# A hybrid encoder layer on one core: the second part of each weight block is made by GpSimd where the lanes run

## The chip, the core and the metric

The kernel runs on one core of a Trainium2 chip. The core has a matrix engine (TensorE, in the profile PE, with its weight loads as PEld), a vector engine (VectorE, DVE), a scalar engine (ScalarE, ACT), a general engine of parallel processors (GpSimd, POOL) and an engine that only issues transfers (SyncE, SP). The metric is the device time of one execution in microseconds, as the median of several.

## What is computed

One layer of a bidirectional encoder with three parallel groups of heads, on two requests (1024 and 256 tokens of width 2048) that share the weights:

```
def layer(x, mem, ...):
    proj = rms_norm(x, norm_g) @ w_in
    xbc, z_ssd, dt_raw, q, k, v, z_att, mq, z_mem = split_cols(proj, IN_SIZES)
    xs, Bm, Cm = split(silu(centred_dwconv(xbc)))
    y = ssd_scan(xs, forward) + ssd_scan(xs, backward) + d_skip * xs
    o_ssd = rms_norm(y * silu(z_ssd))
    o_att = window_attention(rms_norm(q), rms_norm(k), v, sink) * silu(z_att)
    mk, mv = split(rms_norm(mem) @ w_mem_kv)
    o_mem = softmax(rms_norm(mq) @ rms_norm(mk).T) @ mv * silu(z_mem)
    return x + concat[o_ssd, o_att, o_mem] @ w_out
```

Everything is in 32-bit floats.

## The kernel before

**Split products.** TensorE multiplies in a rounded 32-bit form. To keep the precision, each operand is taken in two parts: the rounded part, and the block less its rounded part. A product is then three matmuls: rounded by rounded, rounded by rest, rest by rounded. For the weights this is done block by block by `wsplit`: a block of 128 rows and up to 512 columns lies in a tile `wraw`; ScalarE copies it into `wh` (line 202, the rounding is in the type), and then the second part `wl = wraw - wh` is formed (line 203). The tokens' parts `xH` and `xL` stay on chip, 640 tokens at a time.

**Two groups.** The 1280 tokens are run as two groups of 640. In the first group, after the memory's keys and values and the queries, a stage of "seven products" (`block_pair`) works on ten pairs of weight blocks; there GpSimd forms sums of weight blocks (line 1171), and splits are made of both the blocks and the sums. Then come `kv`, `mq`, `z0`, `z1` of the first group and all the weight blocks of the second, and the output product. The last part of the output product is once more a stage of seven products.

**Blocks.** `block_tok` holds one weight block column of up to 512 wide against five token tiles: 16 steps of 15 matmuls (lines 254 to 256), with the last two steps taken together tile by tile, so that each tile can be evicted in turn. `block_feat` turns the roles round and holds 256 weight columns against the 640 tokens: 8 steps of 24 matmuls (lines 289 to 291). Raw blocks have four buffers (RB), `wh` and `wl` three each (WB): a block can be split as soon as TensorE has released the one three steps before.

**Lanes.** From the end of the first seven-product stage on, the rest of the layer runs beside the weight blocks, in two "lanes" of generators: the windowed attention (`attn`, `k_prep`), the memory attention (`mem_attn`, `mk_prep`), the scan in both directions (`ssd_up`, `ssd_down`, `dt_prep`), and the convolutions (`left`). After each step of a weight block `pump` advances the lanes by a fixed rate for that block. A lane's step brings work for all engines, TensorE too: the transposes of the attention's probabilities (lines 664 and 759) wait for VectorE's scaling of them (lines 652 and 751).

**Order on the engines.** Each engine works through its own queue in order. The order is made at build time from priorities; `wsplit` has a raised one. What a lane step issues is put behind the last weight split, on the engines of that split, by the two instructions that `wsplit` leaves in `marks`:

```
for ins in marks:
    st.enter_context(tc.issue_after(ins))
next(gen)
```

**GpSimd** does little while the lanes run: the reciprocal square roots of the norms (`rsqrt`, lines 120 and 121, and line 1044), and a few masks. SyncE issues nearly all transfers.

Of the kernel before, what the change touches and what calls it, by code (L numbers as in the profile page):

```python
# [10 lines left out]
F32 = mybir.dt.float32  # L11
# [5 lines left out]
ALU = mybir.AluOpType  # L17
# [26 lines left out]
def hymba_encoder_kernel(  # L44
# [7 lines left out]
    V, A, G, T, S = nc.vector, nc.scalar, nc.gpsimd, nc.tensor, nc.sync  # L52
# [88 lines left out]
    def step(lane):  # L141
        name, gen = lane[0]
        try:

            with ExitStack() as st:
# [3 lines that stand above are left out]
        except StopIteration:  # L149
            lane.popleft()  # L150
            done.add(name)
# [3 lines left out]
    def pump(rates):  # L155

        for i in range(2):
            owed[i] = owed[i] + rates[i] if lanes[i] else 0.0
        while max(owed) >= 1:
            i = turn[0] ^ 1  # L160
            i = turn[0] = i if owed[i] >= 1 else i ^ 1
            owed[i] -= 1
            if lanes[i]:
                step(lanes[i])
# [32 lines left out]
            V.scalar_tensor_tensor(out=l, in0=ch, scalar=gain, in1=h.bitcast(F32), op0=ALU.mult, op1=ALU.subtract)  # L197
        yield

    def wsplit(raw, h, l):  # L200

        a = A.activation(h, raw, AF.Copy)  # L202
        b = V.tensor_sub(l, raw, h.bitcast(F32))  # L203
        marks[:] = a.ins, b.ins

    def w_laid(src, n):
# [5 lines left out]
    def laid_in(name):  # L212
        o, n, tok_ = W_AT[name]
        flat = w_in_laid[o:o + D * n]
        return flat.rearrange("(k p c) -> k p c", p=P, c=n if tok_ else 512)
# [7 lines left out]
    def w_out_rows(c):  # L223
        return w_laid(w_out_laid[c], 512)
# [5 lines left out]
    def block_tok(w, nt, evac, before_last=None, feats=range(KT), places=range(KT)):  # L230

        load, n = w
        ps = [acc.tile([P, 512], F32, tag="acc", name="acc") for _ in range(nt)]
        hls = {}
        for k in range(KT):
            raw = wp.tile([P, 512], F32, tag="wraw", name="wraw", bufs=RB)
            load(feats[k], raw[:, :n])
            with tc.high_priority(offset=HP[2]):
                h = wp.tile([P, 512], F32R, tag="wh", name="wh", bufs=WB)
                l = wp.tile([P, 512], F32R, tag="wl", name="wl", bufs=WB)  # L240
                wsplit(raw[:, :n], h[:, :n], l[:, :n])
            hls[k] = h, l
            if k == KT - 2:
                continue
            if k == KT - 1 and before_last is not None:
                before_last(k)

            for t in range(nt):
                for k_ in ((k - 1, k) if k == KT - 1 else (k,)):
                    q, m = divmod(places[k_], 4)  # L250
                    h, l = hls[k_]
                    sh = cur["H", q][:, m, t * P:(t + 1) * P]
                    sl = cur["L", q][:, m, t * P:(t + 1) * P]
                    T.matmul(ps[t][:, :n], sh, h[:, :n], start=(k_ == 0), stop=False)  # L254
                    T.matmul(ps[t][:, :n], sh, l[:, :n], start=False, stop=False)  # L255
                    T.matmul(ps[t][:, :n], sl, h[:, :n], start=False, stop=(k_ == KT - 1))  # L256
                if k == KT - 1:
                    with tc.high_priority(offset=HP[0]):
                        evac(t, ps[t])
            if k == KT - 1:  # L260
                yield k - 1
            yield k

    def block_feat(name, evac):

        ps = [[acc.tile([P, 512], F32, tag="acc", name="acc") for _ in range(2)] for _ in range(2)]
        src = laid_in(name)
        hls = {}
        for kk in range(KT // 2):
            raw = wp.tile([P, 512], F32, tag="wraw", name="wraw", bufs=RB)  # L270
            S.dma_start(raw, src[kk])
            with tc.high_priority(offset=HP[2]):
                h = wp.tile([P, 2, 256], F32R, tag="wh", name="wh", bufs=WB)
                l = wp.tile([P, 2, 256], F32R, tag="wl", name="wl", bufs=WB)
                wsplit(raw, h.rearrange("p a c -> p (a c)"), l.rearrange("p a c -> p (a c)"))
            hls[kk] = h, l
            if kk == KT // 2 - 2:
                continue
            tail = kk == KT // 2 - 1

            for kks in ([(kk - 1, kk)] if tail else [(kk,)]):
                for f in range(2):
                    for k in [2 * x + j for x in kks for j in range(2)]:
                        q, m = divmod(k, 4)
                        sh, sl = [x[:, k % 2, f * P:(f + 1) * P] for x in hls[k // 2]]
                        for half in range(2):
                            c = slice(half * 320, half * 320 + 320)
                            o = ps[f][half][:, :320]
                            T.matmul(o, sh, cur["H", q][:, m, c], start=(k == 0), stop=False)  # L289
                            T.matmul(o, sh, cur["L", q][:, m, c], start=False, stop=False)  # L290
                            T.matmul(o, sl, cur["H", q][:, m, c], start=False, stop=(k == KT - 1))  # L291
                    if tail and f == 0:
                        with tc.high_priority(offset=HP[1]):
                            evac(0, ps[0])
            for k in range(2 * kks[0], 2 * kk + 2):
                yield k
        with tc.high_priority(offset=HP[1]):
            evac(1, ps[1])
# [99 lines left out]
    def ev_out(c0):  # L398
        def f(t, ps):

            if t in (0, 3):
                yt = rp.tile([P, 640], F32, tag="ch", name="yt", bufs=CH)[:, :512]
            else:
                yt = ev.tile([P, 512], F32, tag="evt" if t == 2 else "evu", name="yt")
            S.dma_start(yt, xrow(t)[:, c0:c0 + 512])
            V.tensor_add(yt, ps, yt)
            S.dma_start(y_first[t * P:(t + 1) * P, c0:c0 + 512], yt)
        return f
# [656 lines left out]
    raw, sums, rows = {}, {}, {}  # L1065
# [46 lines left out]
    def beside_step(j):  # L1112
        with ExitStack() as st:
            for ins in marks:
                st.enter_context(tc.issue_after(ins))
            for f, *args in sorted(plan.get(j, ()), key=lambda x: (x[0] is seven_load, x[1])):
                f(*args)
# [350 lines left out]
    queue(0, x_stats, [0])  # L1468
    queue(0, x_rows, [0])
    run(block_tok(w_mk, 4, ev_mk, places=TURNED), MR[0], hold=8)  # L1470
    V.tensor_scalar(out=vec[:, R_CB:], in0=vec[:, R_CB:], scalar1=0.5, scalar2=None, op0=ALU.mult)
    run(block_tok(w_mem_rows(1), 4, ev_mv, places=TURNED), MR[1], extra=p_step)

    def tok(name, w, evac, after=None, grp=0):
        run(block_tok(w, 5, evac), RATES[grp][name], after)

    def feat(name, b, evac, grp, after=None, extra=None):
        run(block_feat(f"{name}{b}", evac), [r / 2 for r in RATES[grp][name]], after, lag=3, extra=extra)
# [19 lines left out]
    early.close()  # L1498


    cl = beside.enter_context(tc.tile_pool(name="cl", bufs=1))
    mp = beside.enter_context(tc.tile_pool(name="mp", bufs=2))
    upper = lconst([P, P], "upper")
# [84 lines left out]
    for c in range(2, 4):  # L1588
        j0 = 16 * (c - 3)
        for k in block_tok(w_out_rows(c), 5, ev_out(c * 512), before_last=lambda _: beside_step(j0 + 14)):  # L1590
            if j0 + k == -7:

                for x in lanes:
                    while x:
                        step(x)
                beside.close()
                fin = ctx.enter_context(tc.tile_pool(name="fin", bufs=2))
            if j0 + k < -7:
                pump(RATES[1]["o"])
            if k != 14:  # L1600
                beside_step(j0 + k)
# [79 lines left out]
```

## Time and profile before

| | us |
|---|---|
| median of 3 runs | 1804.47 |
| lowest, highest | 1803.84, 1804.49 |
| span of the profiled execution | 1800.7 |
| PE busy in it | 1791.2 |
| VectorE busy | 1244.3 |
| ScalarE busy | 903.0 |
| GpSimd busy | 439.5 |

For the profiled execution only the span is at hand, from its first to its last instruction; a time as the runs are timed is not shown beside it. The time of a run holds what lies around the span as well: the median is 3.8 us above it. The granted clock of TensorE was full throughout. In the profile a row names the line of the kernel, the engine, the operation, what is written and what is read (`out<-in`); "idle before" is the time the engine stood idle just ahead of such instructions, with what ended it. Matmuls overlap in their pipeline, so their durations add up to more than the time they take.

### The profile page before, as it was taken

How to read it: one execution, taken by the hardware profiler on the slowest of the kernel's cores; microseconds unless marked ns; L12 is line 12 of the kernel's file. 1: busy time of each engine (PE TensorE's matmuls, PEld its weight loads, DVE VectorE, ACT ScalarE, POOL GpSimd, SP SyncE). 2: the span in 40 equal slices, each digit the busy share in tenths (PEclk: the TensorE clock that was granted, in tenths of full speed). 3: DMA queues.
4: the chain of work that ended last, by engine and by line, in shares of the span. 5: the costliest groups of instructions: out<-in, count | busy, mean ns of one | idle time of the engine just before them, and what ended most of it. 6: DMA issues, size and time to landing. Idle time of an engine off the chain costs nothing.

```text
span 1800.7 us, 30423 instructions
## 1 busy us (share of the span) xinstructions
PE 1791.2 (99%) x10546; PEld 1606.1 (89%) x10546; DVE 1244.3 (69%) x2422; ACT 903.0 (50%) x2039; POOL 439.5 (24%) x714
## 2 busy tenths in 40 slices
PE   9999999999999999999999999999999999999999
PEld 7789999999887899999989987887898888889999
DVE  5595788877657978775755866666885654866665
ACT  6554455444445756564435646544574533543332
POOL 0105789961110000000000000001100000058775
PEclk9999999999999999999999999999999999999999
DMA  8664455446544644444436355457785564644442
GB/s 291 198 179 120 138 153 146 129 136 218 164 136 147 184 134 140 121 132 134 119 96 192 110 161 180 128 178 235 231 266 168 184 190 138 216 153 147 142 143 80
DMA packets 198891, 290.58 MB, mean 161 GB/s; under 512 B 18960, under 2 KB 80464, under 8 KB 198736
## 3 DMA queue, kind: packets, MB, share of 16 engines
q1 hardware_dynamic: 198592, 288.57, 52.7%
q8 instruction: 83, 1.36, 0.3%
q14 instruction: 72, 0.59, 0.1%
q10 hardware_dynamic: 144, 0.06, 0.0%
HBM read 231.12 MB, written 57.44 MB: 160 GB/s over the span
## 4 chain that ended last, share of the span: by engine, by line
PE 61%; DVE 1%; ACT 1%; issue 1%; DMA 1%; POOL 0%; POOLq 0%; ACTq 0%; DVEq 0%
PE acc L254 9%; PE acc L256 8%; PE acc L255 8%; PE acc L289 5%; PE acc L291 5%; PE acc L290 5%; PE acc L1199 3%; PE acc L1201 3%; PE acc L1200 3%; PE py L931 2%; PE po L674 1%; PE ppt L664 1%; PE accm L1200 1%; PE accm L1201 1%; PE accm L1199 1%
## 5 line engine op out<-in xcount | busy, mean ns | idle before, releaser
L203 DVE TENSOR_TENSOR wl<-wraw,wh 128x512 fp32r<-128x512 f32 (+1 forms) x480 | 338.9, 708 | 241.3 <-ACT wh L202 230.7
L254 PE MATMUL acc<-wh,xH 128*128 128x512 f32 (+1 forms) x1248 | 481.9, 386 | 0.2 <-ACT mkr L416 0.2
L255 PE MATMUL acc<-wl,xH 128*128 128x512 f32 (+1 forms) x1248 | 472.2, 378 | 0.9 <-DVE wl L203 0.6
L256 PE MATMUL acc<-wh,xL 128*128 128x512 f32 (+1 forms) x1248 | 472.8, 379 | 0.0
L202 ACT ACTIVATE wh<-wraw 128x512 fp32r<-128x512 f32 (+1 forms) x480 | 292.4, 613 | 323.5 <-PE acc L256 173.3
L254 PEld LDWEIGHTS acc<-wh,xH 128*128 128x128 f32 x1248 | 234.5, 188 | 45.1 <-issue 4.8
L255 PEld LDWEIGHTS acc<-wl,xH 128*128 128x128 f32 x1248 | 234.7, 188 | 43.8 <-DVE wl L203 3.3
L256 PEld LDWEIGHTS acc<-wh,xL 128*128 128x128 f32 x1248 | 234.2, 188 | 43.9 <-issue 0.9
L289 PE MATMUL acc<-xH,wh 128*128 128x320 f32 x640 | 204.5, 320 | 0.0
L291 PE MATMUL acc<-xH,wl 128*128 128x320 f32 x640 | 198.6, 310 | 0.0
L290 PE MATMUL acc<-xL,wh 128*128 128x320 f32 x640 | 198.3, 310 | 0.0
L203 DVE TENSOR_TENSOR sl<-ws,sh 128x384 fp32r<-128x384 f32 x144 | 99.6, 695 | 96.9 <-ACT sh L202 96.6
L202 ACT ACTIVATE sh<-ws 128x384 fp32r<-128x384 f32 x144 | 74.6, 523 | 176.5 <-POOL ws L1171 81.5
L1171 POOL TENSOR_TENSOR ws<-wraw 128x128 f32<-128x128 f32 x144 | 91.1, 633 | 202.0 <-DMA wraw<-in_w_in_pairs_dram 83.6
L289 PEld LDWEIGHTS acc<-xH,wh 128*128 128x128 f32 x640 | 120.3, 188 | 4.1 <-issue 3.7
L290 PEld LDWEIGHTS acc<-xL,wh 128*128 128x128 f32 x640 | 120.3, 188 | 2.6 <-issue 2.2
L291 PEld LDWEIGHTS acc<-xH,wl 128*128 128x128 f32 x640 | 120.1, 188 | 0.7 <-issue 0.6
L1171 POOL TENSOR_TENSOR ws<-wraw,ws 128x128 f32<-128x128 f32 x144 | 93.5, 649 | 11.3
L358 DVE SCALAR_TENSOR_TENSOR c<-u,vec,c 128x638 f32<-128x638 f32 (+1 forms) x96 | 88.6, 926 | 10.0 <-ACT c L353 9.7
L1171 POOL TENSOR_TENSOR ws<-ws,wraw 128x128 f32<-128x128 f32 x144 | 94.2, 654 | 0.0
L120 POOL TENSOR_SCALAR qr<-qss 128x8 f32<-128x8 f32 x10 | 4.3, 428 | 366.6 <-DVE qss L598 366.6
L1171 POOL TENSOR_TENSOR wraw<-wraw 128x128 f32<-128x128 f32 x144 | 89.2, 620 | 11.1
(427 smaller groups left out, 3645.1 us busy)
## 6 DMA issues: line engine op xcount, KB each, us to landing
wraw<-in_w_in_laid_dram SPq DMA_DIRECT2D x208, 256.0 KB, 2.8
wraw<-in_w_in_pairs_dram SPq DMA_DIRECT2D x80, 256.0 KB, 2.8
wraw<-in_w_out_laid_dram SPq DMA_DIRECT2D x64, 256.0 KB, 3.5
wraw<-in_w_out_pairs_dram SPq DMA_DIRECT2D x64, 256.0 KB, 2.8
rf<-ac SPq DMA_DIRECT2D x40, 256.0 KB, 3.7
rb<-ac SPq DMA_DIRECT2D x40, 256.0 KB, 4.1
wraw<-in_w_mem_laid_dram SPq DMA_DIRECT2D x32, 256.0 KB, 4.8
xst<-in_x_sample_dram SPq DMA_DIRECT2D x20, 256.0 KB, 4.7
```

Source lines behind the costliest of these rows:

```text
L202: a = A.activation(h, raw, AF.Copy)
L203: b = V.tensor_sub(l, raw, h.bitcast(F32))
L254: T.matmul(ps[t][:, :n], sh, h[:, :n], start=(k_ == 0), stop=False)
L255: T.matmul(ps[t][:, :n], sh, l[:, :n], start=False, stop=False)
L256: T.matmul(ps[t][:, :n], sl, h[:, :n], start=False, stop=(k_ == KT - 1))
L289: T.matmul(o, sh, cur["H", q][:, m, c], start=(k == 0), stop=False)
L290: T.matmul(o, sh, cur["L", q][:, m, c], start=False, stop=False)
L291: T.matmul(o, sl, cur["H", q][:, m, c], start=False, stop=(k == KT - 1))
L358: V.scalar_tensor_tensor(out=c[0], in0=u[:, k:k + n], scalar=cw[k], in1=c[0], op0=ALU.mult, op1=ALU.add)
L1171: G.tensor_tensor(out=o, in0=x, in1=y, op=op)
L1199: T.matmul(ps[p], h, xh, start=(k_ == 0), stop=False)
L1200: T.matmul(ps[p], h, xl, start=False, stop=False)
```

## The change

A one-element list `low` holds the engine that forms the second part in `block_tok` and `block_feat`. It starts as VectorE, is set to GpSimd after the first seven-product stage, just before the lanes' pools are opened, and back to VectorE in the third block of the output product, when the lanes have been emptied and their pools are closed. `wsplit` takes the engine as an argument; the seven-product stages call it without, and so keep VectorE. The subtraction is the same, and `marks` now holds ScalarE's and GpSimd's instruction where the engine is GpSimd.

```
+    low = [V]
+
-    def wsplit(raw, h, l):
+    def wsplit(raw, h, l, low=V):
 
         a = A.activation(h, raw, AF.Copy)
-        b = V.tensor_sub(l, raw, h.bitcast(F32))
+        b = low.tensor_tensor(out=l, in0=raw, in1=h.bitcast(F32), op=ALU.subtract)
         marks[:] = a.ins, b.ins
...
     def block_tok(...):
-                wsplit(raw[:, :n], h[:, :n], l[:, :n])
+                wsplit(raw[:, :n], h[:, :n], l[:, :n], low[0])
...
     def block_feat(...):
-                wsplit(raw, h.rearrange("p a c -> p (a c)"), l.rearrange("p a c -> p (a c)"))
+                wsplit(raw, h.rearrange("p a c -> p (a c)"), l.rearrange("p a c -> p (a c)"), low[0])
...
     early.close()
+    low[0] = G
     cl = beside.enter_context(tc.tile_pool(name="cl", bufs=1))
...
                 beside.close()
+                low[0] = V
                 fin = ctx.enter_context(tc.tile_pool(name="fin", bufs=2))
```

## The prediction

> **What bounds the kernel now.** I read the busy table, then the stretch in which the change acts, then the waits of that stretch engine by engine, and last single rows of the timeline.
>
> ```profile
> PE 1791.2 (99%) x10546; PEld 1606.1 (89%) x10546; DVE 1244.3 (69%) x2422; ACT 903.0 (50%) x2039; POOL 439.5 (24%) x714
> ```
> ```profile
> 393.00:1516.00 1123.00, 1120.15 (x6552) 979.64 (x6551) 771.00 (x1676) 579.47 (x1436) 68.13 (x108) 1.00 0.54 163
> ```
> ```profile
> PE pmt L759 <- DVE mpr L751: 1.3, 2, 0.8
> PE ppt L664 <- DVE lg L652: 0.9, 2, 0.5
> PE po L674 <- ACT so L995: 0.3, 1, 0.3
> PE psc L632 <- ACT qT L618: 0.2, 1, 0.2
> ```
>
> The second row is the sum of engine time from 393 to 1516 us, from the first weight block after the seven-product stage to the reset of the engine. Its columns are PE, weight loads, VectorE, ScalarE and GpSimd. PE is busy for 1120.15 of 1123.00 us, at full granted clock, so its idle time is 2.85 us. The PE waits of the stretch, the next four rows, add up to 2.7 us, and none of them is for a weight block: `wl` is never late. VectorE has 352 us idle (1123.00 - 771.00), GpSimd 1055 us. TensorE sets the time here, and an edit on VectorE or GpSimd counts only as far as PE comes to wait, or stops waiting.
>
> **What is moved.**
>
> ```profile
> 146.00:393.00 247.00, 117.31 (x157) 1.00 0.48 140
> 393.00:1516.00 1123.00, 175.96 (x267) 1.00 0.54 163
> ```
> ```profile
> L203 DVE TENSOR_TENSOR wl<-wraw,wh 128x512 fp32r<-128x512 f32 x235 | 161.5, 688 | 156.2 <-ACT wh L202 147.1 <-DMA rb<-ac 3.5 <-DMA xc<-xbc_d 2.7
> ...
> L203 DVE TENSOR_TENSOR wl<-wraw,wh 128x288 fp32r<-128x288 f32 x32 | 14.7, 458 | 24.1 <-ACT wh L202 23.9
> ```
>
> These are the subtractions of line 203 in that stretch. One of the 267 belongs to the stage before; by the code 266 move (64 in the rest of the first group, 160 in the second, 42 in the output blocks): 234 of 512 columns and 32 of 288. VectorE loses 234 x 0.688 + 32 x 0.458 = 175.7 us of work. None of it is on the path, so this alone brings 0.
>
> **What one costs on GpSimd.** No row of before shows a 512-column subtraction there. The nearest:
>
> ```profile
> L1171 POOL TENSOR_TENSOR ws<-wraw x144: 453/465/1963, 47.4 to 1782.3; 128x128 f32<-128x128 f32 x144
> ```
> ```profile
> 209.05 0.77 POOL L1171 TENSOR_TENSOR ws<-ws,wraw 128x128 f32<-128x128 f32 x1
> ```
> ```profile
> 209.42 0.94 DVE L203 TENSOR_TENSOR wl<-wraw,wh 128x512 fp32r<-128x512 f32 x1
> ```
>
> 128 columns take 0.465 us in the median of the least disturbed kind. A VectorE subtraction that began while GpSimd was at such a one took 0.94 us where it takes 0.688 alone: 0.25 us more. I read that as the time GpSimd needs the shared reading, 2.0 ns a column. Then 512 columns take 0.465 + 384 x 0.0020 = 1.23 us, and 288 take 0.78. The bounds are 0.465 (no growth with width) and 4 x 0.465 = 1.86 us (all of it grows). I take 1.23, nearer to the middle, since the stretch of 0.25 us is measured. GpSimd gets 234 x 1.23 + 32 x 0.78 = 313 us more: 381 of 1123 us, 34%. Even at four times the 128-column cost (some 540 us in all) it keeps up.
>
> The Trainium skill (GPSIMD Engine Reference, Elementwise — side-by-side cycle accounting) gives about 2.6 cycles an element at 1.2 GHz for a two-input operation, which is 1.11 us for 512 as an estimate, and says elementwise work belongs on VectorE; by it the sum below would be the same.
>
> **Is the block still in time?**
>
> ```profile
> ACT wh L202 <- PE acc L256: 137.7, 69, 4.5
> ```
> ```profile
> 503.69 0.61 ACT L202 ACTIVATE wh<-wraw 128x512 fp32r<-128x512 f32 x1
> ...
> 507.03 0.62 ACT L202 ACTIVATE wh<-wraw 128x512 fp32r<-128x512 f32 x1
> ...
> 510.68 0.62 ACT L202 ACTIVATE wh<-wraw 128x512 fp32r<-128x512 f32 x1
> ```
> ```profile
> 425.12 0.44 ACT L202 ACTIVATE wh<-wraw 128x288 fp32r<-128x288 f32 x1 [1.53 <-PE acc L256]
> ...
> 425.60 0.46 DVE L203 TENSOR_TENSOR wl<-wraw,wh 128x288 fp32r<-128x288 f32 x1 [1.47 <-ACT wh L202]
> ...
> 427.42 0.29 PE L255 MATMUL acc<-wl,xH 128*128 128x288 f32 x1
> ```
>
> ScalarE makes `wh` when PE releases a buffer (first row). There are three (WB), so a block is split while PE has two others to multiply. Steps are 3.3 to 3.7 us apart (next three rows), so some 6 us stay after `wh` ends. The tightest place I found is the last block of the narrow weight (last three rows): `wh` ends at 425.56 and PE reads `wl` at 427.42, 1.86 us later. There GpSimd needs 0.78 us, and with one VectorE instruction of 0.9 us ahead of it at the shared reading 1.7. It fits, by little. Elsewhere 1.23 + 0.9 = 2.1 us fit easily. GpSimd's queue is also emptier than VectorE's, where `wl` stood in line behind lane work. I put this at 0; the far end is 32 narrow steps late by 0.1 to 0.2 us, 4 us.
>
> **What VectorE gains and loses.**
>
> ```profile
> DVE wl L203 <- ACT wh L202: 171.0, 108, 4.2
> ...
> DVE yd L984 <- POOL yrs L1044: 14.0, 8, 2.2
> ...
> DVE kr L488 <- POOL krr L121: 7.3, 8, 1.1
> ...
> DVE q L604 <- POOL qr L121: 1.8, 1, 1.8
> ```
> ```profile
> L203 DVE TENSOR_TENSOR wl<-wraw,wh 128x512 fp32r<-128x512 f32 x80 | 67.3, 847 | 11.4 <-ACT wh L202 11.2
> ```
> ```profile
> L358 DVE SCALAR_TENSOR_TENSOR c<-u,vec,c 128x638 f32<-128x638 f32 x37 | 36.6, 991 | 0.1
> ```
> ```profile
> L358 DVE SCALAR_TENSOR_TENSOR c<-u,vec,c 128x646 f32<-128x646 f32 x48 | 42.3, 887 | 9.8 <-ACT c L353 9.7
> ```
>
> VectorE's queue stood 171.0 us behind subtractions that waited for ScalarE. That wait moves to GpSimd, and lane work behind it (convolutions, softmax, SSD products) may start earlier. The cost is contention. From 146 to 393 us, where GpSimd forms weight sums, the subtraction takes 847 ns against 688, and the convolution tap (L358) 991 against 887 though its rows are 8 columns shorter. In the new stretch GpSimd would hold the reading for 266 x about 1.0 us, 24% of the time, half a microsecond on average for whoever meets it: 0.12 us for each VectorE instruction that reads two SBUF operands. If all 1409 that remain did, that were 169 us, less than the 175.7 removed. So VectorE ends no busier than before and I book 0, between a gain of its queue's freedom and that loss.
>
> The Trainium skill (SBUF — State Buffer, Who interferes with whom) says the pair is locked for a whole instruction, against any VectorE instruction with two SBUF inputs, and the second to come blocks fully; the 0.94 us above agrees in kind.
>
> The square-root pairs of lines 120 and 121 now queue on GpSimd behind a subtraction that itself may wait for `wh`, and line 984, 488 and 604 wait for them (23.1 us in the rows above). 44 such chains at one subtraction each, 44 x 1.23 = 54 us, lie in VectorE's 352 us idle: 0. If that cover fails it is part of the first rival. The order of issue also loosens: a lane step is held behind the last split on the engines of that split, which now are ScalarE and GpSimd, no longer VectorE. SP's queue and its loads stay as they are; `wraw` is released within a microsecond of before.
>
> **Sum.** The profiled execution spans 1800.7 us; no time of its own is shown beside it. The median of the runs is 1804.47 us, 3.8 above the span, and I carry that 3.8 over. The terms are 0 (work removed), 0 (block in time), 0 (VectorE) and +0.5 for a few new PE waits of the sort that already cost 2.2 us. 1800.7 + 3.8 + 0.5 = 1805.0 us.
>
> **The rivals.**
>
> ```profile
> L652 DVE TENSOR_SCALAR lg<-lg,den 128x384 f32<-128x384 f32 x48 | 17.9, 415 | 0.2
> ...
> L751 DVE TENSOR_SCALAR mpr<-mpr,mden 128x256 f32<-128x256 f32 x40 | 12.4, 350 | 0.6
> ...
> L652 DVE TENSOR_SCALAR lg<-lg,den 128x256 f32<-128x256 f32 x32 | 9.8, 348 | 0.1
> ```
> ```profile
> 1348.57 0.61 DVE L652 TENSOR_SCALAR lg<-lg,den 128x256 f32<-128x256 f32 x2
> ```
> ```profile
> 1349.06 0.63 PE L664 MATMUL ppt<-identr,lg 128*128 128x128 f32 x4 [0.46 <-DVE lg L652]
> ```
>
> *Slower: the lanes' probabilities come late.* PE's queue is in order, and at 100 places it transposes what VectorE has just scaled (80 by L652, 20 pairs by L751). In the last two rows PE has waited 0.46 us and starts while the second of the two scalings is still running: no margin there, and behind that transpose stand the weight matmuls. A chain to such a place has about two instructions that would need the shared reading; 2 x 0.12 us is 0.24 us, times 100 is 24 us if every place is bare. For it: that row. Against it: only 4 waits of this kind are recorded (2 and 2 in the PE rows above), and a `wl` of 0.69 us no longer cuts into the chain. With a third of the places bare it is 8 us: 1812.5; with all, 1828.5. It decides from 0.04 us a place on (3.6 us in all). The square-root chains, if they hold VectorE up at the wrong moment, work through the same places. The locking rule named above, taken at its full word, is this rival's upper end: a VectorE instruction that meets a subtraction of 1.23 us waits out the rest of it.
>
> *Slower: the block itself is late.* The cost lies near 1.86 us, and 1.86 + 0.9 passes the 1.86 us margin of the narrow blocks: 0.5 + 4 us, 1808.5 us. From about 1.0 us a narrow subtraction on. Against it: only two blocks are narrow, and one step was that tight.
>
> *Faster: the freed VectorE takes waits away.* Without `wl` the lanes' results stand ready earlier. What can be won is PE's idle time in the stretch, 2.85 us, and whatever waits hide in the pipelined matmuls: I allow as much again, 5 us at most, 1799.5 us; typically 4: 1800.5.
>
> That the change does nothing can be left out: the engine is named outright at both callers and set back only in the third output block.
>
> **How the numbers follow.** Two runs of this kernel can be told from no change from about 0.2% on, 3.6 us: faster is below 1800.9, slower above 1808.1. The forecast case, all terms covered, has 0.44, and its own range is 1801 to 1808. Late probabilities 0.36, late blocks 0.05, freed VectorE 0.15. So faster 0.15, same 0.44, slower 0.41. The range takes in the faster case down to 1799 and late probabilities up to two thirds of their full price (0.5 + 24 x 0.67 is about 16, less 4 us for what the absent `wl` gives back): 1817. What lies above and below has less than 2 in 10.
>
> **What would show it.** GpSimd's subtraction of 512 columns at 1.1 to 1.4 us undisturbed and up to 2.2 where VectorE is in its way; GpSimd some 380 us busy between 393 and 1516 us; VectorE's busy time there at 600 to 770 us, with no wait on `wh` from line 203; taps of L358 above 887 ns; PE idle still about 3 us, and no PE wait on a GpSimd `wl` over 0.5 us. The forecast is wrong if PE's waits for `ppt`, `pmt` or the like sum to over 4 us, if `acc` L255 or L291 waits for GpSimd's `wl`, if one subtraction takes 1.9 us or more, or if PE's idle time falls and the span with it.

## The result, and the profile after

The changed kernel takes 1854.11 us (median of four runs, 1853.76 to 1855.18) where the kernel before, with one more run, takes 1804.15 us: a ratio of 1.0281, interval 1.0267 to 1.0296. That is 49 us above the forecast of 1805.0 and far outside its range. The profiled execution took 1854.25 us and spans 1852.5 us, 51.8 more than before.

The page's busy line, then the list of cores, then the stretch in which the change acts (from the first weight block after the seven-product stage to the reset of the engine; columns as in the prediction):

```profile
PE 1808.6 (98%) x10546; PEld 1615.0 (87%) x10546; DVE 1209.1 (65%) x2156; ACT 901.0 (49%) x2039; POOL 779.7 (42%) x980
```
```profile
core 0: 1852.5 us, clock 0.993
```
```profile
397.00:1566.00 1169.00, 1134.71 (x6535) 986.21 (x6536) 728.02 (x1402) 576.57 (x1435) 408.68 (x371) 0.99 0.52 156
```

46.0 of the 51.8 us arise here (1169.00 against 1123.00). VectorE is busy for 728.02 us, 43 less than before, and GpSimd for 408.68, so neither is a bound by its sum. Yet PE is idle for 1169.00 - 1134.71 = 34.3 us, where it was 2.9: 31.4 of the 46.0 us. The other 14.6 are PE's own busy time, and the granted clock of 0.993 tells what most of it is.

PE's waits over the whole execution (what was waited for; us, times, longest):

```profile
PE ppt L666 <- DVE lg L654: 6.8, 8, 3.1
PE pmt L761 <- DVE mpr L753: 6.5, 4, 2.7
PE psc L634 <- DVE lg L636: 3.3, 2, 1.7
PE acc L256 <- DVE dt_all L334: 2.5, 1, 2.5
PE pms L741 <- DVE mql L726: 2.4, 3, 1.4
PE pst L860 <- DVE bl L902: 2.3, 1, 2.3
...
PE acc L257 <- POOL wl L205: 0.5, 1, 0.5
```

PE waits for a block of GpSimd's once, 0.5 us. It waits for VectorE: the rows of this view that name VectorE add up to 35.4 us (4.7 before). The first two are the probabilities of the first rival. The next four are other lane work: scores whose PSUM buffer VectorE has not yet emptied (L634), the scan's step sizes, the rounded rest of the queries, the scan's B. Each is one to three waits, the longest of them 1.4 to 2.5 us, not many small ones.

What is late is seen in the groups of GpSimd and of VectorE (duration of all, mean ns of one):

```profile
L205 POOL TENSOR_TENSOR wl<-wraw,wh 128x512 fp32r<-128x512 f32 x234 | 319.0, 1365 | 620.6 <-ACT wh L204 570.8 <-PE acc L293 6.7 <-PE pyf L876 6.1
...
L205 POOL TENSOR_TENSOR wl<-wraw,wh 128x288 fp32r<-128x288 f32 x32 | 28.0, 876 | 52.3 <-ACT wh L204 48.9 <-DMA rf<-ac 3.3
```
```profile
L360 DVE SCALAR_TENSOR_TENSOR c<-u,vec,c 128x646 f32<-128x646 f32 x48 | 56.3, 1176 | 8.8 <-ACT c L355 7.9
...
L636 DVE SCALAR_TENSOR_TENSOR lg<-ndist,psc 128x384 f32<-128x384 bf16 x48 | 24.9, 545 | 18.7 <-PE psc L635 18.7
L654 DVE TENSOR_SCALAR lg<-lg,den 128x384 f32<-128x384 f32 x48 | 24.3, 547 | 0.4
L639 DVE TENSOR_REDUCE m<-lg 128x2 f32<-128x768 f32 x24 | 22.6, 943 | 0.1
```

The convolution's tap, with two operands in SBUF, takes 1176 ns instead of 887. The scaling of the probabilities (L654; L652 before) takes 547 instead of 415. L636, with one operand in PSUM, and the reduction L639 stay at what they were (548 and 946 ns).

The timeline shows how such means become waits (start, duration, engine, line; in brackets the idle time just before):

```profile
819.56 1.58 POOL L205 TENSOR_TENSOR wl<-wraw,wh 128x512 fp32r<-128x512 f32 x1 [2.99 <-ACT wh L204]
...
819.91 1.93 DVE L360 SCALAR_TENSOR_TENSOR c<-u,vec,c 128x646 f32<-128x646 f32 x1
...
823.70 0.88 DVE L360 SCALAR_TENSOR_TENSOR c<-u,vec,c 128x646 f32<-128x646 f32 x1
...
826.54 1.40 POOL L205 TENSOR_TENSOR wl<-wraw,wh 128x512 fp32r<-128x512 f32 x1 [5.40 <-ACT wh L204]
...
826.77 1.71 DVE L938 TENSOR_TENSOR ya<-ya,sk 128x512 f32<-128x512 f32 x1
828.41 0.61 DVE L753 TENSOR_SCALAR mpr<-mpr,mden 128x256 f32<-128x256 f32 x2
...
828.89 0.63 PE L761 MATMUL pmt<-identr,mpr 128*128 128x128 f32 x4 [0.97 <-DVE mpr L753]
```

A tap that begins while GpSimd is at its subtraction takes 1.93 us; the next one, alone, 0.88. L938 meets the following subtraction and takes 1.71 us (0.69 before). Right behind it in VectorE's queue stands the scaling for which PE has stopped: 0.97 us, almost exactly what L938 lost.

The tap ends 0.70 us after the subtraction that it met (821.84 and 821.14). That is the rule in this trace: of the 48 taps of this shape, 17 began while a subtraction was running, and each ended 0.69 us after the end of the one that it met first; they took 0.97 to 1.95 us. Ten others met a subtraction that began after them and took their usual 0.88 to 0.89. So the second to come stands still until the first is through, and it loses the rest of the subtraction, less 0.2 us.

And the clock, in three windows around the longest wait, 3.1 us:

```profile
622.00:626.00 4.00, 0.90 (x6) 0.44 (x5) 3.90 (x12) 2.54 (x7) 0.00 (x0) 1.00 0.24 89
626.40:629.80 3.40, 3.40 (x12) 3.02 (x11) 2.25 (x6) 3.29 (x9) 0.65 (x1) 0.50 0.29 96
629.80:633.00 3.20, 3.20 (x19) 2.70 (x18) 3.06 (x6) 2.13 (x4) 0.63 (x1) 1.00 0.22 82
```

While PE stands (0.90 of 4.00 us busy), VectorE works through 3.90 of 4.00 us. Then PE gets half the clock for 3.4 us and does 12 matmuls; in the 3.2 us behind them, at full clock, it does 19. In the stretch the granted clock drops to 0.50 six times, five times for 3.4 us and once for 6.8. PE is busy for 22.6 of these 23.8 us, so the half rate costs some 11.3 us (an estimate: half of the busy time), most of the 14.6. Before, the clock was full throughout. The five short drops follow waits of 1.75 to 3.1 us. The long one comes 2 us after the wait of 0.97 us shown above, in the middle of the next wait for the same kind of scaling (2.69 us). The seven other waits of 1.26 to 1.74 us in the stretch were followed by none. The Trainium skill (TensorE: Matmul & The Clock Gate, Why this matters for your kernels) advises against PE-idle gaps over about 3 us; here a gap of 1.75 us was enough. The unit of 3.4 us agrees with the activity window that the same page of the Trainium skill gives (TensorE: Matmul & The Clock Gate, Part 1: The HAM clock gate).

What decides can be read from the trace. The six drops start at 397.68, 442.05, 626.37, 715.12, 831.17 and 1315.86 us, whole multiples of 3.413 us apart, so on one grid in time. In the piece of that grid just ahead of each drop PE was busy for 0.55 to 1.56 of 3.41 us; in every other piece at full clock, up to the last of the execution, it was busy for 1.67 us or more. The two that lie nearest, with a drop behind the first alone:

```profile
394.26:397.68 3.42, 1.56 (x9) 1.25 (x9) 2.56 (x4) 0.58 (x2) 1.24 (x1) 1.00 0.46 139
735.60:739.01 3.41, 1.67 (x11) 1.41 (x11) 3.38 (x5) 0.12 (x1) 1.39 (x1) 1.00 0.12 32
```

So it is not one wait's length that counts, but how much of one such piece PE stands idle.

### The profile page after: what moved, and what is told of

Read it like the earlier page. It is cut to its first block, busy times and chain, and to the rows that moved or that the text cites. A ratio compares the mean times of both kernels' runs of the same rounds, so it can differ in the third digit from the quotient of the medians.

```text
span 1852.5 us, 30493 instructions
## 1 busy us (share of the span) xinstructions
PE 1808.6 (98%) x10546; PEld 1615.0 (87%) x10546; DVE 1209.1 (65%) x2156; ACT 901.0 (49%) x2039; POOL 779.7 (42%) x980
## 5 line engine op out<-in xcount | busy, mean ns | idle before, releaser
L205 POOL TENSOR_TENSOR wl<-wraw,wh 128x512 fp32r<-128x512 f32 (+1 forms) x266 | 347.0, 1306 | 673.0 <-ACT wh L204 619.7
L205 DVE TENSOR_TENSOR wl<-wraw,wh 128x512 fp32r<-128x512 f32 x214 | 163.2, 766 | 61.2 <-ACT wh L204 57.7
L360 DVE SCALAR_TENSOR_TENSOR c<-u,vec,c 128x638 f32<-128x638 f32 (+1 forms) x96 | 104.7, 1094 | 9.0 <-ACT c L355 7.9
L1173 POOL TENSOR_TENSOR ws<-wraw,ws 128x128 f32<-128x128 f32 x144 | 95.1, 661 | 11.3
```

The costliest lines, as they stand in the source:

```text
L205: b = low.tensor_tensor(out=l, in0=raw, in1=h.bitcast(F32), op=ALU.subtract)
L360: V.scalar_tensor_tensor(out=c[0], in0=u[:, k:k + n], scalar=cw[k], in1=c[0], op0=ALU.mult, op1=ALU.add)
L1173: G.tensor_tensor(out=o, in0=x, in1=y, op=op)
```

## The experiments

Times stand against runs of the kernel before on the same chip: 1802.83 us for the two experiments on the order, for GpSimd's reading alone and for the quarters; 1801.58 for the memsets on the raw tile, for the zeros without the mark and for the pieces with the mark; 1802.39 for the zeros with the mark and for the additional steps. The stretch rows have the columns of the window rows above. "VectorE's stretch" is its busy time in that row, less the 595.0 us that it has before without the subtractions (771.00 - 175.96), less what the kernel itself adds.

**The order alone.** The subtraction stays on VectorE, but a lane step is held behind ScalarE's instruction only, as after the change VectorE no longer carries the second mark.

```
-        marks[:] = a.ins, b.ins
+        marks[:] = (a.ins, b.ins) if low is V else (a.ins,)      # low is G while the lanes run; b is VectorE's
```

> The subtraction stays on VectorE; only the loosened order is taken from the change: while the lanes run, a lane step is held behind the split on ScalarE alone, no longer on VectorE. Theory contention (GpSimd's subtraction holds the reading that it shares with VectorE, VectorE's lane results come late, and PE waits in its queue): no GpSimd work is added, so 1804 us, within 3. Theory order (lane work is issued earlier than VectorE can serve it; the attention's transposes stand up to 18 weight matmuls earlier in PE's queue): most of the 50 us, 1830 to 1854 us.

Measured: 1806.74 us, ratio 1.0021 (1.0012 to 1.0031).

```profile
394.00:1518.00 1124.00, 1118.99 (x6535) 976.86 (x6536) 765.76 (x1668) 577.66 (x1435) 68.19 (x107) 1.00 0.54 163
```

PE is idle for 5.0 us and the clock is full. The looser order costs about 4 us of the 50.

**The order put back.** The changed kernel, with a copy of one column on VectorE that waits for `wh`, as the subtraction did, and serves as the mark.

```
         marks[:] = a.ins, b.ins
+        if low is G:
+            tick = sm.tile([P, 1], F32, tag="tick", name="tick", bufs=4)
+            marks.append(V.tensor_copy(tick, h[:, :1].bitcast(F32)).ins)
```

> The changed kernel, with the old order given back: after each split on GpSimd a VectorE copy of one column of wh is added (266 of about 0.16 us), and lane steps are held behind it on VectorE as they were behind the subtraction before. Theory contention: the loss stays, 1845 to 1865 us. Theory order: the loss goes, 1804 to 1812 us.

Measured: 1846.99 us, ratio 1.0246 (1.0229 to 1.0264).

```profile
392.00:1556.00 1164.00, 1133.66 (x6550) 986.92 (x6549) 783.73 (x1675) 579.01 (x1437) 409.25 (x374) 0.99 0.52 157
```

With VectorE's order back, 44 of the 50 us remain. The order is a small part of the loss, not its cause.

**GpSimd's reading alone.** The kernel before, and behind each split a second subtraction on GpSimd, whose result nobody uses; from the first blocks of the second group to the third output block, 194 of the 266 splits.

```
         b = V.tensor_sub(l, raw, h.bitcast(F32))
+        if twice:
+            G.tensor_tensor(out=rbc[:, :l.shape[-1]], in0=raw, in1=h.bitcast(F32), op=ALU.subtract)
```

> The kernel before, subtraction and order on VectorE as they were, but from the second convolution block to the third output block (194 splits) GpSimd makes the same subtraction once more, into a tile that nobody reads. Theory contention: those blocks lost 32 us in the changed kernel, and here VectorE keeps its own subtraction too, so at least 30 us: 1834 us or more, with PE waits on VectorE of the same kinds. Theory order: 1804 to 1808 us, since no lane step is loosened.

Measured: 1863.72 us, ratio 1.034 (1.0325 to 1.0356).

```profile
393.00:1575.00 1182.00, 1139.20 (x6545) 989.12 (x6544) 882.65 (x1674) 575.91 (x1437) 363.21 (x300) 0.99 0.51 155
```
```profile
L208 POOL TENSOR_TENSOR rbc<-wraw,wh 128x512 f32<-128x512 f32 x178 | 280.1, 1574 | 504.4 <-ACT wh L204 392.9 <-issue 93.7 <-DMA rb<-ac 5.6
```
```profile
L362 DVE SCALAR_TENSOR_TENSOR c<-u,vec,c 128x646 f32<-128x646 f32 x48 | 52.9, 1108 | 9.3 <-ACT c L357 9.1
```

Nobody reads this result, VectorE keeps its subtractions and the marks are as before; yet the loss is there, larger than the change's. VectorE's same instructions take 882.65 us instead of 771.00. Of the first group's blocks, in which nothing was added, four that were compared by the start of their first matmul lost less than 0.7 us each.

**The same time on GpSimd without reading.** The kernel before, with three memsets of the block's raw tile on GpSimd behind each of the same 194 splits.

```
+        if twice:
+            for _ in range(3):
+                G.memset(raw, 0.0)
```

> As the experiment with a second subtraction beside (order and subtraction on VectorE, 194 splits), but GpSimd fills the spent raw block with zeros three times in place of subtracting: about 1.5 us of GpSimd a block, estimated from 205 ns for 128 columns, and nothing read. Theory contention by the shared reading: 1803 to 1810 us, against 1863.7 with reading. If the writing side is held against VectorE too (its copies and scalings at double rate write through both): 1820 to 1845 us.

Measured: 1805.62 us, ratio 1.0018 (1.0008 to 1.0028).

```profile
394.00:1519.00 1125.00, 1120.32 (x6545) 978.34 (x6544) 777.22 (x1674) 579.25 (x1436) 365.57 (x687) 1.00 0.53 163
```
```profile
L209 POOL MEMSET wraw<- 128x512 f32 x534 | 283.4, 532 | 473.1 <-DVE wl L205 420.5 <-issue 13.9 <-ACT bh L889 7.8
```
```profile
L363 DVE SCALAR_TENSOR_TENSOR c<-u,vec,c 128x646 f32<-128x646 f32 x48 | 42.3, 887 | 9.4 <-ACT c L358 9.2
```

GpSimd is as busy as in the run before this (365.57 and 363.21 us), behind the same splits, but it only writes. (The memsets begin after VectorE's subtraction of the block, the reading beside it; in the next experiment the memsets begin where the change's subtractions do.) The tap keeps its 887 ns, VectorE takes 777.22 us, the clock is full, and 4 us are lost, not 61 (what these 4 are was not taken apart). These two runs are the core of the case: it is GpSimd's reading of SBUF that costs. It agrees with the Trainium skill (SBUF — State Buffer, Who interferes with whom), by which a VectorE instruction with two SBUF inputs contends with a GpSimd instruction that reads SBUF, and not with one that only writes.

Reading does a second thing, which these two runs do not separate from the first: it keeps the block's buffers. ScalarE's next copy into `wh` has to wait until GpSimd has read what lies there. The rows, in order, are from the change, from the run with reading alone, and from the kernel with quarters, further below; before, and with memsets, ScalarE has no such waits.

```profile
ACT wh L204 <- POOL wl L205: 18.4, 13, 2.8
ACT wh L204 <- POOL rbc L208: 21.6, 9, 4.0
ACT wh L204 <- POOL wl L207: 23.2, 13, 3.4
```

Whether this is what makes PE wait can be read from the traces. In the change, from 617 us on, PE has twelve waits of 0.9 us or more in the stretch. In the 8 us ahead of each, ScalarE had no wait for GpSimd of more than 0.2 us, and during the waits themselves VectorE was busy for 20.5 of 21.9 us. In the quarters ScalarE waits longer than in the change, and the loss is smaller. Only the two waits ahead of these, at 395 and 439 us, have such a wait of ScalarE's within 8 us, so its part there is open.

**VectorE's relief alone.** The second part is left out while the lanes run: GpSimd fills `wl` with zeros, which needs no reading. In a second kernel the mark on VectorE is put back as well.

```
+        if low is G:
+            b = G.memset(l.bitcast(F32), 0.0)
+        else:
+            b = V.tensor_tensor(out=l, in0=raw, in1=h.bitcast(F32), op=ALU.subtract)
```

> The changed kernel, but GpSimd fills wl with zeros in place of the subtraction (what is left out: the second part of the weights while the lanes run). VectorE is as free and the order as loose as in the change, and GpSimd writes as often, but reads nothing. Theory contention by the shared reading: the loss goes; what is left is the loosened order, 1802 to 1808 us, and PE waits on VectorE under 8 us. If writing or GpSimd being busy at all is what costs: 1820 us or more.

> Zeros in place of the subtraction on GpSimd (left out: the second part of the weights while the lanes run), and the old order given back by the one-column copy on VectorE. If the loosened order is what costs the 4 us in the two kernels that have it without the contention: 1800 to 1803 us, ratio 0.999 to 1.001. If those 4 us come from elsewhere: 1805 to 1808 us.

Measured: 1806.22 us, ratio 1.0024 (1.0014 to 1.0033), and with the mark 1802.54 us, ratio 1.0001 (0.9992 to 1.001; of its eleven times one, 10149.31 us, is not in the ratio).

```profile
394.00:1518.00 1124.00, 1118.14 (x6537) 977.05 (x6536) 624.90 (x1405) 577.25 (x1435) 197.89 (x373) 1.00 0.53 163
```
```profile
393.00:1516.00 1123.00, 1117.94 (x6542) 978.02 (x6541) 649.80 (x1674) 579.86 (x1435) 196.43 (x372) 1.00 0.53 163
```

VectorE has 146 and 121 us less to do than before, and nothing is won. The 4 us of the first of the two are gone with the mark: the size of the order's own price in the first experiment. So the best that the change could have brought was zero.

**Shorter readings.** The changed kernel, each subtraction in four pieces of 128 columns.

```
+        n = l.shape[-1]
+        for c in [slice(0, n)] if low is V else [slice(i * n // 4, (i + 1) * n // 4) for i in range(4)]:
+            b = low.tensor_tensor(out=l[:, c], in0=raw[:, c], in1=h[:, c].bitcast(F32), op=ALU.subtract)
```

> The changed kernel with GpSimd's subtraction cut into four of 128 columns, so the same reading in four holds of about 0.25 us in place of one of 1.0 (GpSimd's time rises from 1.3 to 1.9 us a block). Contention by a hold for the whole instruction: a VectorE instruction waits at most a quarter as long at a time and gets in between, so the loss about halves: 1820 to 1835 us. Contention by shared bandwidth: the read time is the same, 1850 us or more. Theory order: as the change, 1850 to 1858 us.

Measured: 1832.17 us, ratio 1.0162 (1.0147 to 1.0177).

```profile
395.00:1544.00 1149.00, 1128.42 (x6534) 980.24 (x6533) 678.03 (x1403) 577.46 (x1435) 608.33 (x1164) 1.00 0.52 159
```
```profile
L362 DVE SCALAR_TENSOR_TENSOR c<-u,vec,c 128x646 f32<-128x646 f32 x48 | 46.1, 962 | 10.3 <-ACT c L357 9.5
```

GpSimd is busy for 608 us instead of 409 and reads the same data, but the loss falls from 50 to 29 us. VectorE's stretch falls from 133 us (728.02 - 595.0) to 83, the tap from 1176 to 962 ns. Between these two kernels it is how long one reading holds VectorE up that decides, not how long GpSimd is busy.

**Shorter readings with the mark.** Four pieces, and eight of 64 columns, each with the mark on VectorE.

```
+        n, m = l.shape[-1], 1 if low is V else 8       # 4 in the first of the two
+        for i in range(m):
+            c = slice(i * n // m, (i + 1) * n // m)
+            b = low.tensor_tensor(out=l[:, c], in0=raw[:, c], in1=h[:, c].bitcast(F32), op=ALU.subtract)
```

> The changed kernel with both remedies: four pieces of 128 columns and the old order given back by a one-column copy on VectorE. If the gains add (22 us from the pieces, 7 from the order): 1825 us. If the order only mattered because of long holds: 1830 to 1834 us. Either theory leaves it above 1804.

Measured: 1842.23 us, ratio 1.0224 (1.0206 to 1.0242). It missed what was expected: with whole subtractions the mark took the loss from 50 to 44 us, with quarters it takes it from 29 to 41.

```profile
392.00:1552.00 1160.00, 1129.85 (x6549) 983.36 (x6548) 712.24 (x1675) 579.34 (x1437) 619.63 (x1168) 1.00 0.52 158
```
```profile
L212 DVE COPY tick<-wh 128x1 f32<-128x1 f32 x266 | 39.5, 149 | 209.7 <-ACT wh L204 208.7
```

VectorE once more stands idle ahead of copies that wait for `wh` (209.7 us), and PE now waits 6.9 us for GpSimd's blocks (1.6 without the mark). VectorE's stretch, without its copies, is 712.24 - 595.0 - 39.5 = 78 us, hardly less than without the mark. Why the order's sign turns was not settled.

> As before, in eight pieces of 64 columns: holds of about 0.13 us, GpSimd about 2.7 us a block (8 x 0.33). Hold per instruction: the waits of VectorE shrink again, 1812 to 1822 us, unless GpSimd now is late with the block itself: in the narrow blocks and at block ends (1.9 us from the end of wh to the first use) PE would wait for GpSimd's wl, 10 to 20 us. Shared bandwidth: no better than in four pieces.

Measured: 1887.22 us, ratio 1.0472 (1.0456 to 1.0488), far above all that was expected.

```profile
393.00:1597.00 1204.00, 1143.08 (x6540) 989.60 (x6540) 685.60 (x1674) 576.26 (x1436) 805.34 (x2228) 0.98 0.50 152
```
```profile
L208 POOL TENSOR_TENSOR wl<-wraw,wh 128x64 fp32r<-128x64 f32 x1872 | 673.4, 395 | 328.8 <-ACT wh L204 290.8 <-DMA rb<-ac 6.5 <-PE acc L299 6.4
```
```profile
PE acc L263 <- POOL wl L208: 19.7, 13, 4.0
PE ppt L672 <- DVE lg L660: 11.3, 6, 5.7
PE pmt L767 <- DVE mpr L759: 8.9, 2, 7.1
```

The contention shrinks further (the tap is at 916 ns), but a second loss appears. Eight pieces of 0.395 us make 3.2 us a block, where the steps are 3.3 to 3.7 us apart, and PE waits 19.7 us for blocks, of 60.9 us that it is idle in the stretch. The waits at the transposes grow too, to 20.2 us in the two rows above; why was not taken apart (ahead of the longest, 7.1 us, VectorE itself stood for 5.2 us, by the profile for a transfer). So of the sizes tried, whole, four pieces and eight (eight with the mark only), four did best, and they still lost 29 us.

**More room ahead of the transposes.** If only the places were bare at which PE transposes what VectorE has just scaled, a step more between the two should take the loss away. The changed kernel, with an additional `yield` ahead of each of the six places where the attentions turn probabilities, and the first lane's rates raised by 15% to make up for it; beside it the kernel before with the same edit.

```
+        yield
         turn_(...)
...
-RATES = ({'kv': (2.0, 1.0), ...
+RATES = ({'kv': (2.30, 1.0), ...
```

> The changed kernel with one more lane step ahead of each transposing of the probabilities (four in the window attention, two in the memory attention) and the first lane's rates raised by 15% to keep its pace. Theory bare places (PE's transposes follow VectorE's scaling too closely, so its lateness becomes PE idle time): waits for ppt and pmt, 13.3 us in the change, fall below 5, and with the clock drops they cause the time to 1825 to 1842 us. Rival (VectorE is late by whole microseconds in all lane work, so the waits only move to other places): 1846 us or more.

> The same added steps and rates in the kernel before, as the control: its lanes have few waits to lose (2.2 us for ppt and pmt) and the pace is kept, so 1800 to 1810 us by either theory.

Measured: 1849.03 us, ratio 1.0262 (1.0248 to 1.0276); the kernel before with the edit 1804.23 us, ratio 1.0013 (1.0004 to 1.0022).

```profile
PE ppt L666 <- DVE lg L654: 6.7, 8, 1.5
PE pms L745 <- DVE mql L730: 4.9, 2, 3.1
PE psc L634 <- DVE lg L636: 3.6, 3, 1.6
PE pst L865 <- ACT pT L667: 2.6, 1, 2.6
```

PE's waits at the transposes fall from 16.1 to 9.0 us, all releasers taken together, and those at other places rise from 23 to 31: scores, the queries' rest, the scan. The loss stays at 47 us. The theory of a few bare places falls; all lane work runs late, and PE meets it at whichever place comes next.

## Why the prediction was wrong

**What bounds the kernel, and the price of GpSimd's work, were right.** One subtraction was put at 1.23 us (0.78 for the narrow ones) and took 1.365 and 0.876; the sum, put at 313 us, was 347; GpSimd, put at 381 us, was busy for 408.68.

**"Is the block still in time": right for TensorE.** It was booked at 0 and cost one PE wait of 0.5 us. It was not asked whether ScalarE, which needs the buffer back, would wait for GpSimd: it did, for 18.4 us in all.

**"What VectorE gains and loses": this step failed.** Its mean was good: 0.12 us for each of VectorE's instructions was estimated, and 133 us over 1402 make 0.095. VectorE did end less busy than before. From that a 0 was booked, and this does not follow. The stretch does not come as 0.1 us everywhere, but as up to 1 us on a few instructions (1.93 for 0.88, 1.71 for 0.69; 31 of the 48 taps lost nothing), and PE waits for single chains, not for a sum. VectorE's 440 us of idle time in the stretch are no cover for a chain that is late by 1 us at the moment when PE's queue reaches it. The gain set against it, VectorE's freed time, is worth nothing by the runs in which the subtraction was left out: subtracting a gain without worth from a loss with a price gave the 0.

**The first rival had the mechanism and the wrong size.** It said that the lanes' probabilities come late, at 8 us in the middle and 24 at most. It was sized by the mean (two times 0.12 us a place) and by 100 places of one kind. At those places PE waited 16.1 us; the other 23 us of its waits lie elsewhere (the scores' buffers, the queries' rest, the scan's inputs), where the rival did not look. What it named as its upper end, that an instruction waits out the rest of the subtraction that it meets, is what the taps do. The run with more room showed that this is one lateness, not a list of places.

**The clock was missing altogether.** No term had it. Some 11.3 us of the 51.8 are six drops to half rate behind PE's waits. The sum that should have been made, of the traces: 31.4 us more idle and 11.3 at half rate in the stretch, 3.3 of matmuls that are longer for reasons not taken apart, and 5.8 outside it, of which 4.0 lie ahead of its start (a wait of 1.75 us at its edge among them).

**"The order of issue also loosens"** was told without a price. Alone it costs 4 us, and with the contention it goes either way: putting the order back gained 6 us with whole subtractions and cost 11 with quarters. So it belonged in the range. One of its places is known. PE's waits for VectorE's own subtractions in the seven-product stages come to 1.7 to 2.4 us in every kernel without the mark on VectorE, and to 0.2 to 0.8 in every kernel with it. In the change the longest of these is the wait of 1.75 us at the stretch's edge, and the first drop of the clock follows it; with the order alone the longest is 1.2 us, and the clock stays full.

**Two slips in the sums,** neither of which decides. The 3.8 us that were carried from the span to the time are not what lies around a span: in every run that has both, the time is 1.7 to 2.1 us above it, so some 2 us of the 3.8 are the difference between two executions. And the late blocks, at 0.5 + 4 us, come to 1809.0 us, not 1808.5.

**Of the signs,** the ones that were to tell the forecast wrong did: waits for `ppt` and `pmt` over 4 us, PE idle far from 3 us. Two more came without weight: one wait for GpSimd's `wl` (0.5 us), and single subtractions over 1.9 us (the longest 2.54). Taps above 887 ns, VectorE between 600 and 770 us, and no VectorE wait on `wh` in the stretch came as forecast. "Faster" had 0.15 for a freed VectorE and is excluded: with 121 us less on VectorE and the old order, the ratio was 1.0001.

## What to carry to other kernels

Work moved from VectorE to GpSimd is priced by what GpSimd's reading does to single VectorE instructions with two SBUF operands, up to about 1 us for a meeting with a 512-column subtraction here, and by who stands behind them in the queue; the sum of busy times said the opposite of the result. Where TensorE is busy to 99% and its queue is in order, ask how late one chain can get, not how late the mean is, and add the clock: a wait of 2 or 3 us cost 1.7 us more at half rate (half of 3.4). Before moving work off an engine, find out what the relief is worth by leaving the work out: here it was 0, and one run shows it.

## What the runs showed of the hardware

- GpSimd busy for 366 us with memsets left the tap at 887 ns; busy for 363 us with reading subtractions it made it 1108. The writing was not wholly free: the scaling of 384 columns went from 415 to 466 ns beside the memsets (547 beside the subtractions of the change).
- GpSimd's subtraction has a large fixed part: 395 ns for 64 columns and 1365 for 512, both as means in company, so some 260 ns (estimated by a line through the two) before the first column.
- A VectorE tap that began while GpSimd's subtraction ran ended 0.69 us after that subtraction (17 of 17 in the change); one that began first kept its 0.88 to 0.89 us (10 of 10). With memsets all 34 taps that met one stayed at 0.87 to 0.90 us.
- The granted clock fell to half for 3.4 us at points of one grid of 3.413 us, each time after a piece of the grid in which PE was busy for 0.55 to 1.56 us; pieces with 1.67 us or more at full clock were followed by none (the change, without the end of the execution). The long drop went on after a piece at half clock with 2.1 us busy. In the other runs the border lies between 0.43 and 0.54 of a piece, so it is about half.
